# A four-layer trunk: feature-major products for SwiGLU, DeltaNet and RWKV's receptance, a triangle product for the RWKV decay, and the first norm's shift and scale in two halves

## The chip, the cores and the metric

The kernel runs on one core of one Trainium2 chip. The metric is the device time of one execution in microseconds (us); a run's time is compared with that of the kernel before on the same chip. The engines are TensorE (PE, with its weight loads shown as PEld), VectorE (DVE), ScalarE (ACT), GpSimd (POOL) and SyncE (SP, which only issues DMAs here). TensorE writes its products to PSUM, which has eight banks of 128 x 512 fp32.

## The reference, cut to what matters

Two streams of 128 tokens and 1024 features (a context and a latent) pass four layers. Each layer is a token mixer (DeltaNet, neighbourhood attention, latent attention, RWKV) and a SwiGLU FFN, each as `x += gate * f(rmsnorm(x) * (1 + scale) + shift)`. All arrays are fp32.

```python
mp = jnp.split(s_ctx @ ada_w[l] + ada_b[l], 6, -1)      # shift, scale, gate; shift, scale, gate
hp = modulate(rmsnorm(yp, norm_mix[l]), mp[0], mp[1])
...
q, k, v, z = jnp.split(h @ w_in, 4, -1)                 # DeltaNet, 4 x 1024 columns
qkv = jax.nn.silu(dwconv_centred(jnp.concatenate([q, k, v], -1), conv_w))   # 3 taps along the tokens
...
w = -jax.nn.softplus(-(w0[:, None, None, :] + lora(xm[3], w1, w2, jnp.tanh))) - 0.5   # RWKV, two directions
decay = jnp.exp(-jnp.exp(w.astype(F32)))
...
yp = yp + mp[5] * swiglu(modulate(rmsnorm(yp, norm_ffn[l]), mp[3], mp[4]), ffn_w_in[l], ffn_w_out[l])
```

The FFN goes from 1024 to 2 x 2816 features and back. The two streams are the two "groups" s = 0 and 1 below.

## The kernel before, in words

**Recording and planning.** The kernel's methods don't issue instructions; they record them on a tape (class Tape, line 64). Plan (line 1652) gives every instruction an estimated cost, orders all of them over the five engines by a list schedule with priorities (forwards, line 1787; backwards, line 1927), repeats this ROUNDS = 9 times with WAIT = 1800 ns (how long an engine may be kept for a more urgent instruction), and trunk_kernel (line 2040) issues the order with the shortest planned end. emit (line 2009) issues every instruction from one line, so all rows of the trace have line 2032 and all tiles the name v; groups are told apart by shape. Tiles come from fixed pools (ROOM, line 501): 25 of 1024 columns, 28 of 512, three of 2048 for ada_w, and 7 + 1 PSUM banks.

**Products in fp32r.** A weight block of 2 x 128 rows and 512 columns is loaded by SP and split into hi and lo (split, line 261: a ScalarE copy to fp32r and a VectorE subtraction, both 1024 columns). linear (line 296) holds the normalised tokens (128 features x 128 tokens of one group, hi and lo) stationary and streams 512 weight columns. For each row block k and group s it issues three products, x_hi w_hi, x_hi w_lo and x_lo w_hi, into one bank, 128 tokens x 512 features. Group 0 runs some steps ahead of group 1 (order, line 284; lags FIN, IN). linear_k (line 323) does the same over rows for FFN-out, with 2 x 2 banks. Plain fp32 products (RWKV's projections, the ada products) go through PE in two passes, each a matmul of its own in the trace; an fp32r product and a transpose are one.

**FFN** (ffn_, line 453). Chunks of 512 hidden features come in pairs, value and gate; the SiLU of the first is kept, the second multiplied by it, and to_T (line 360) turns the 128 x 512 result round with four PE transposes before it is split into hi and lo as the stationary operand of FFN-out: 11 x 4 = 44 transposes of 128 x 128 a layer.

**DeltaNet** (deltanet_, line 637). After the norm come a gate product (24 fp32r products, weights stationary, 256 columns of tokens) and linear over eight chunks: q, k, v and z, two chunks each. evac (line 733) copies a q, k or v chunk of one group from its bank, transposes it to feature-major (4), applies the three taps (per 128 features one ScalarE copy and two VectorE operations over 127 tokens), a SiLU, transposes back (4) and copies; q and k also get their squares summed. Then the triangular inverse for all heads runs on VectorE as one chain of 62 small operations between two pairs of 1024-wide stream transposes (inverse_base and substitute, lines 519 and 535).

**Shift and scale** (ada_group, line 217). A group g is 2048 of the 6144 columns of ada_w[l]: for each of eight row blocks four products, 32 rows of conditions stationary, 512 columns each, side by side in four column groups of the array. Group 0 of layer 0 is made in setup (line 176) from 16 loads of 1024 columns; the others by fill (line 1989), one 2048-column load for a row block, after each mixer's projections.

**RWKV** (rwkv_, line 1188). project (line 1283) makes k, r and v as plain fp32 products through linear_k, 512 columns each; features (line 1296) transposes r (16). rw_decays (line 1402) makes, for a half g of the features and a direction d, the decay's pre-activation by products of 64 rows x 256 columns, a tanh, an addition, a running sum along the tokens by two VectorE scans of 512, a subtraction of the value at the middle token, and exponentials. A half's keys, products and triangular inverse follow; the second half's inverse comes late in the layer.

Of the kernel before, what the change touches and what calls it, by code (L numbers as in the profile page):

```python
# [96 lines left out]
class Trunk:  # L97
# [78 lines left out]
    def setup(self):  # L176
# [18 lines left out]
        self.ada_group(0, 0, 1024, "b")  # L195
# [21 lines left out]
    def ada_group(self, l, g, width=2048, kind="ada"):  # L217
# [8 lines left out]
        n = width // 512  # L226
        for k in range(KD):
            for h in range(4 // n):
                w = self.g([128, width], kind=kind)
                at = g * 2048 + h * width  # L230
                nc.sync.dma_start(w, I["ada_w"][l, k * 128:(k + 1) * 128, at:at + width])
                for i in range(n):
                    j = h * n + i
                    nc.tensor.matmul(p[32 * j:32 * j + 32, :], self.cT[:, k, :], w[:, i * 512:i * 512 + 512],
                                     start=(k == 0), stop=(k == KD - 1), tile_position=(0, 32 * j))
                self.free(w)
# [13 lines left out]
    def ada_col(self, l, part, s):  # L250

        n = 2 * part
        return self.ada[l][:, n // 4, :, s].rearrange("p (c j) -> p j c", j=4)[:, n % 4:n % 4 + 2]
# [68 lines left out]

    def linear_k(self, W, xs, evac, lags=None, done=None, whole=False):
# [54 lines left out]
    def normed(self, l, which, s, more=None):  # L378
# [4 lines left out]
        with self.scope():  # L383
# [3 lines left out]
            nc.vector.scalar_tensor_tensor(gs, self.ada_col(l, 3 * which + 1, s), 1.0,  # L387
                                           self.gcol[:, which, l, :].rearrange("p (j c) -> p j c", j=2),
                                           op0=OP.add, op1=OP.mult)
            sh = self.ada_col(l, 3 * which, s)  # L390
            for g in range(2):
                xn = self.g([128, 512])
# [9 lines left out]
                yield g, p, gs[:, g, :], sh[:, g, :]  # L402
# [50 lines left out]
    def ffn_(self, l):  # L453
# [5 lines left out]
        chunks = []  # L459
        for c in range(5):  # L460
            chunks += [[(c * 512, c * 512 + 512)], [(FF + c * 512, FF + c * 512 + 512)]]
        chunks += [[(2560, FF), (FF + 2560, 2 * FF)]]
        sil = {}

        def evac(ci, s, ps):
            if ci < 10 and ci % 2 == 0:
# [6 lines left out]
            with self.scope():  # L473
                m = self.g([128, 512])
                if ci < 10:
                    nc.vector.tensor_tensor(m, ps, sil[s], op=OP.mult)
                    self.free(sil[s])
                    n = 4
                else:
                    t = self.g([128, 512])  # L480
                    nc.scalar.activation(t[:, :256], ps[:, :256], AF.Silu)
                    nc.vector.tensor_tensor(m[:, :256], ps[:, 256:], t[:, :256], op=OP.mult)
                    n = 2
                self.to_T(m, n, hid[c][0][:, :n, s, :], hid[c][1][:, :n, s, :])
        self.linear(W, chunks, xs, evac, FIN)
# [23 lines left out]
ROUNDS = 9  # L509
WAIT = 1800.0  # L510
# [5 lines left out]
class DeltaNet:  # L516
# [120 lines left out]
    def deltanet_(self, l):  # L637
# [95 lines left out]
        def evac(ci, s, ps):  # L733
            which, half = ci // 2, ci % 2
            if which == 3:
                nc.scalar.activation(zs[s][half].rearrange("p a b -> p (a b)"), ps, AF.Silu)
                return
            with self.scope():
                tok = self.g([128, 512])
                nc.scalar.activation(tok, ps, AF.Copy)  # L740
                p = self.ps()
                for i in range(4):
                    nc.tensor.transpose(p[:, i * 128:(i + 1) * 128], tok[:, i * 128:(i + 1) * 128], self.ident)
                x = p.rearrange("p (a b) -> p a b", b=128)
                cv = self.g([128, 4, 128])
                for i in range(4):
                    c = ci * 4 + i
                    nc.scalar.activation(cv[:, i], x[:, i], AF.Copy, scale=cw[:, 1, c:c + 1])
                    nc.vector.scalar_tensor_tensor(cv[:, i, 1:], x[:, i, :127], cw[:, 0, c:c + 1], cv[:, i, 1:], op0=OP.mult, op1=OP.add)
                    nc.vector.scalar_tensor_tensor(cv[:, i, :127], x[:, i, 1:], cw[:, 2, c:c + 1], cv[:, i, :127], op0=OP.mult, op1=OP.add)  # L750
                nc.scalar.activation(cv, cv, AF.Silu)
                p = self.ps()
                for i in range(4):
                    nc.tensor.transpose(p[:, i * 128:(i + 1) * 128], cv[:, i], self.ident)
                h0 = half * 4
                dst = (qk[s][which][:, h0:h0 + 4] if which < 2 else V[s][half]).rearrange("p a b -> p (a b)")
                nc.scalar.activation(dst, p, AF.Copy)
                if which < 2:
                    sq = self.g([128, 512])
                    nc.scalar.activation(sq, p, AF.Square)  # L760
                    nc.vector.tensor_reduce(ss[:, s, which, h0:h0 + 4], sq.rearrange("p (a b) -> p a b", b=128), axis=AX.X, op=OP.add)
            if ci == 3:
                unit(s)
            if ci == 5 and s == 1:
# [34 lines left out]
        self.linear(I["dn_w_in"][j], [[(c * 512, c * 512 + 512)] for c in range(8)], xs, evac, IN)  # L799
# [380 lines left out]
class Rwkv:  # L1180
# [7 lines left out]
    def rwkv_(self, l):  # L1188
# [4 lines left out]
        r = self.g([96, 128])  # L1193
        for at, n, v in ((0, 48, I["rw_mu"][j].rearrange("i (k p) -> (i k) p", p=128)),
                         (48, 8, I["rw_k_a"][j].rearrange("(k p) -> k p", p=128)),
                         (56, 8, I["rw_r_k"][j].rearrange("(k e) d -> k (e d)", e=2)),
                         (64, 16, I["rw_w0"][j].rearrange("z (k p) -> (z k) p", p=128)),
                         (80, 16, I["rw_a0"][j].rearrange("z (k p) -> (z k) p", p=128))):
            nc.gpsimd.dma_start(r[at:at + n], v)
        p = self.ps()  # L1200
        nc.tensor.transpose(p[:, :96], r, self.ident[:96, :96])
        self.free(r)
        cols = self.g([128, 96])
        nc.vector.tensor_copy(cols, p[:, :96])
        mu = cols[:, 0:48].rearrange("p (i k) -> p i k", k=8)

        nc.vector.tensor_scalar(cols[:, 64:96], cols[:, 64:96], 0.5, None, op0=OP.mult)
# [3 lines left out]
        self.rw_b0 = {"w": cols[:, 64:80].rearrange("p (z k) -> p z k", z=2), "a": cols[:, 80:96].rearrange("p (z k) -> p z k", z=2)}  # L1211
# [35 lines left out]
        wa = self.g([128, 2, 2, 128])  # L1247

        def lora(i, nm):
# [14 lines left out]
            t = hid[nm] = wa[:, "wa".index(nm)] if nm != "g" else self.g([128, 2, 128])  # L1264
# [5 lines left out]

        self.seg = self.g([128, 512])
        nc.gpsimd.memset(self.seg, 1.0)
        nc.gpsimd.memset(self.seg[:, ::128], 0.0)
        w2 = [{}, {}]
        for g in range(2):
            for nm in "wa":
                w2[g][nm] = self.g([128, 512])
                nc.gpsimd.dma_start(w2[g][nm], I[f"rw_{nm}2"][j].rearrange("z r n -> (z r) n")[:, g * 512:g * 512 + 512])
# [64 lines left out]
        lora(4, "a")  # L1343
        k = project(1, mk, KLAGS)
# [25 lines left out]
        r = project(0, mr, RLAGS)  # L1370
# [6 lines left out]
        rT = features(r)  # L1377
# [24 lines left out]
    def rw_decays(self, g, d, hid, w2):  # L1402
# [5 lines left out]
        act = {}  # L1408
        for nm in "wa":
            o = self.g([128, 4, 2, 128])  # L1410
            for h in range(2):
                p = self.ps()
                for i in range(2):
                    nc.tensor.matmul(p[:, i * 256:i * 256 + 256], w2[nm][rows, (2 * h + i) * 128:(2 * h + i + 1) * 128],
                                     hid[nm][rows].rearrange("p s t -> p (s t)"), start=True, stop=True, tile_position=(64 * d, 0))
                for i in range(2):
                    c = g * 4 + 2 * h + i
                    nc.scalar.activation(o[:, 2 * h + i].rearrange("p s t -> p (s t)"), p[:, i * 256:i * 256 + 256], AF.Tanh,
                                         bias=self.rw_b0[nm][:, d, c:c + 1], scale=0.5)
            act[nm] = o  # L1420
        sg, al = act["w"], act["a"]
        seq = lambda t: t.rearrange("p c s t -> p (c s) t")

        cm = self.g([128, 4, 2, 128])
        fl = lambda t: t.rearrange("p c s t -> p (c s t)")
        nc.vector.tensor_scalar(fl(sg), fl(sg), 1.0, None, op0=OP.add)
        a, b = (fl(sg), fl(cm)) if d == 0 else (fl(sg)[:, ::-1], fl(cm)[:, ::-1])
        shp = [128, 8, 128]
        for h in (0, 512):
            nc.vector.tensor_tensor_scan(b[:, h:h + 512], self.seg, a[:, h:h + 512], 0.0, op0=OP.mult, op1=OP.add)  # L1430
        mid = self.g([128, 8])
        nc.vector.tensor_copy(mid, seq(cm)[:, :, 63 + d])
# [628 lines left out]
```

## Time and profile before

| | |
|---|---|
| median of 3 runs | 1683.51 us (1679.96 to 1689.08) |
| the profiled execution | 1688.48 us, span 1686.7 us |
| PE busy | 1587.1 us, 9396 matmuls |
| VectorE, ScalarE busy | 1128.2 us, 830.3 us |
| loaded from HBM | 328.25 MB |
| granted TensorE clock, mean | 0.969 |

The profile is of one execution. A matmul's listed duration is its latency; matmuls overlap, so what one costs in a dense run is the step from start to start. "x" stands before a count. Times in timelines are from the span's start; a row there merges matmuls that follow each other and names the first one's shape.

### The profile page before, as it was taken

The numbers are of one execution on the slowest core, as the hardware profiler recorded it, in microseconds if no ns is written. First come the engines' busy times: TensorE is split into PE (matmuls) and PEld (weight loads), VectorE is DVE, ScalarE is ACT, GpSimd is POOL, SyncE is SP. The second block draws the span as 40 slices with busy tenths as digits, with TensorE's granted clock in tenths as the row PEclk, the third lists the DMA queues.
The fourth block names the chain that finished last, engine by engine and source line by source line (L and its number), as shares of the span: only waits on it lengthen the run. The fifth ranks groups of instructions, "written<-read, shape, count | busy, mean of one in ns | idle before, by whom it ended". The sixth has DMA issues, their size and how long they took to land.

```text
span 1686.7 us, 24968 instructions
## 1 busy us (share of the span) xinstructions
PE 1587.1 (94%) x9396; PEld 1206.5 (72%) x9396; DVE 1128.2 (67%) x2364; ACT 830.3 (49%) x1466; POOL 63.3 (4%) x109
## 2 busy tenths in 40 slices
PE   6999689999999899999998999999999499999998
PEld 2877267888767658887775688886657378878886
DVE  4788868545486675445798854548797878675554
ACT  4798166434455664444565644433545432354443
POOL 2001010000002000000000000001010010000000
PEclk9999899999999999999999999999998779999999
DMA  9665888545658684455767854557120452335553
GB/s 364 226 215 195 325 307 319 200 147 183 208 215 269 195 299 158 169 175 204 249 215 255 334 165 174 187 200 253 59 101 10 166 195 82 114 119 178 164 193 130
DMA packets 130601, 333.79 MB, mean 198 GB/s; under 512 B 18321, under 2 KB 32466, under 8 KB 119216
## 3 DMA queue, kind: packets, MB, share of 16 engines
q1 hardware_dynamic: 123888, 311.33, 52.4%
q0 software_dynamic: 6592, 20.86, 4.2%
q8 instruction: 74, 1.21, 0.3%
q14 instruction: 47, 0.39, 0.1%
HBM read 328.25 MB, written 3.90 MB: 197 GB/s over the span
## 4 chain that ended last, share of the span: by engine, by line
PE 73%; DVE 12%; DMA 8%; ACT 5%; issue 2%; SPq 0%; ACTq 0%; DVEq 0%
PE v L2032 73%; DVE v L2032 12%; DMA v<-ada_w 5%; ACT v L2032 4%; DMA v<-ffn_w_out 2%; DMA v<-na_w_qkv 1%; DMA v<-dn_w_in 1%; ACT L2032 0%; DMA v<-ffn_w_in 0%; SPq L2032 0%; ACTq L2057 0%; ACTq L2032 0%; DVEq L2032 0%
## 5 line engine op out<-in xcount | busy, mean ns | idle before, releaser
L2032 PE MATMUL v<-v,v 128*128 128x512 f32 (+13 forms) x9364 | 1582.6, 369 | 94.1 <-DVE v L2032 44.5
L2032 PEld LDWEIGHTS v<-v,v 128*128 128x128 f32 (+6 forms) x9364 | 1200.4, 170 | 473.2 <-issue 148.7
L2032 DVE TENSOR_TENSOR v<-v,v 128x512 f32<-128x512 f32 (+19 forms) x1271 | 864.4, 705 | 477.5 <-ACT v L2032 280.8
L2032 ACT ACTIVATE v<-v 128x512 f32<-128x512 f32 (+9 forms) x989 | 679.1, 721 | 797.2 <-PE v L2032 373.6
L2032 ACT ACTIVATE v<-v,v 128x128 f32<-128x128 f32 (+2 forms) x212 | 77.3, 413 | 30.4 <-PE v L2032 12.5
L2032 DVE SCALAR_TENSOR_TENSOR v<-v,v,v 128x127 f32<-128x127 f32 (+4 forms) x200 | 66.9, 381 | 7.1 <-ACT v L2032 6.1
L2032 ACT ACTIVATE v<-v,v,v 128x128 f32<-128x128 f32 (+2 forms) x136 | 55.4, 476 | 23.6 <-DVE v L2032 23.3
L2032 DVE TENSOR_REDUCE v<-v 128x4 f32<-128x512 f32 (+4 forms) x76 | 47.1, 626 | 18.0 <-PE v L2032 12.9
L2032 POOL DMA_DIRECT2D v<-v x22 | 11.8, 535 | 780.5 <-PE v L2032 633.9
L2032 DVE TENSOR_SCALAR v<-v 128x1 int32<-128x1 int32 (+9 forms) x194 | 32.8, 175 | 9.1 <-ACT v L2032 6.1
L2032 DVE SCALAR_TENSOR_TENSOR v<-v,v 128x1 f32<-128x1 f32 (+7 forms) x156 | 32.6, 218 | 4.8 <-ACT v L2032 2.2
L2032 ACT ACT_TABLE_LOAD x22 | 28.2, 1283 | 2.4 <-DVE v L2032 1.4
L2032 POOL MEMSET v<- 128x512 f32 (+3 forms) x26 | 15.6, 618 | 330.4 <-PE v L2032 182.4
L2032 DVE SCALAR_TENSOR_TENSOR v<-v 128x1 f32<-128x1 f32 (+4 forms) x171 | 26.2, 159 | 2.5
L2032 DVE TENSOR_SCALAR v<-v,v,v 128x128 f32<-128x128 f32 x64 | 25.0, 404 | 2.0 <-PE v L2032 1.5
L2032 DVE STREAM_TRANSPOSE v<-v 128x1024 f32<-128x1024 f32 x12 | 23.4, 2003 | 3.8 <-ACT v L2032 3.6
L2032 DVE TENSOR_SCALAR v<-v,v 128x512 f32<-128x512 f32 (+2 forms) x68 | 24.6, 395 | 0.4
L2032 DVE TENSOR_TENSOR v<-v 128x1 f32<-128x1 f32 (+4 forms) x74 | 11.7, 160 | 10.9 <-ACT v L2032 9.7
L2032 DVE COPY v<-v 128x32 f32<-128x32 f32 (+9 forms) x34 | 7.5, 223 | 12.8 <-PE v L2032 12.6
L2032 ACT ACTIVATION_READ_ACCUMULATOR v<-v,v 128x1 f32 x64 | 13.3, 208 | 0.0
L2032 DVE TENSOR_TENSOR_SCAN v<-v,v 128x512 f32<-128x512 f32 x8 | 9.2, 1206 | 0.1
L2032 PE MATMUL v<-v 128*128 128x256 f32 x32 | 8.0, 378 | 0.0
(39 smaller groups left out, 62.5 us busy)
## 6 DMA issues: line engine op xcount, KB each, us to landing
v<-ada_w SPq DMA_DIRECT2D x88, 1024.0 KB
v<-ffn_w_in SPq DMA_DIRECT2D x160, 512.0 KB
v<-ffn_w_out SPq DMA_DIRECT2D x88, 512.0 KB
v<-dn_w_in SPq DMA_DIRECT2D x32, 512.0 KB
v<-na_w_qkv SPq DMA_DIRECT2D x24, 512.0 KB
v<-rw_w_rkv SPq DMA_DIRECT2D x24, 512.0 KB
v<-v POOLq DMA_DIRECT2D x20, 512.0 KB, 7.0
v<-ada_w SPq DMA_DIRECT2D x16, 512.0 KB
```

The source lines that it names most:

```text
L2032: ins = getattr(getattr(nc, engine), method)(*[real(a) for a in args], **{k: real(a) for k, a in kw.items()}).ins
```

## The change

Five things are edited.

- **linear_T**, new: the weights (hi or lo, 128 x 128) are the stationary operand and the 2 x 128 tokens of both groups the moving one, 256 columns, so that a chunk of 512 features comes out feature-major in two banks. It takes all chunks of the FFN but the first pair (TM = 1), and q, k and v of DeltaNet; z stays with linear. With `early` = 2 the first two DeltaNet chunks are done in two halves of the rows.
- **The evacuations** behind it work on both groups at once: DeltaNet's lose the copy and the first four transposes, the FFN's lose to_T.
- **ada_start**: the first norm's shift and scale come in two halves of the features, each with its own eight loads of 2 x 512 columns, its biases and two column groups of PE; normed takes its scale and shift by halves.
- **RWKV**: r is projected with the weights stationary (project_T) and comes out feature-major; the decay's pre-activation is a token-major product with the bias as a row of ones, and the running sum along the tokens a product with a triangle whose middle column is subtracted beforehand (rw_tri). The value at the middle token is set to 1 by POOL.
- **Planning**: ROUNDS = 14 with each of WAITS = (900, 3000), so 28 orders to choose from.

```diff
-        self.ada_group(0, 0, 1024, "b")
+        self.ada_first = [self.c([128, 4, 2, 2]) for _ in range(2)]
+        for j in range(2):
+            self.ada_start(j)
...
+    def ada_start(self, j):
+        nc, I = self.nc, self.I
+        half = lambda a: a[:, 0:2048].rearrange("k (q j n) -> k q j n", q=2, j=2)[:, :, j]
+        b = self.g([64, 512])
+        nc.gpsimd.memset(b, 0.0)
+        for m in range(2):
+            nc.sync.dma_start(b[m::32], half(I["ada_b"][0:1]).rearrange("o q n -> (o q) n"))
+        p = self.ps()
+        for k in range(KD):
+            w = self.g([128, 2, 512])
+            nc.sync.dma_start(w, half(I["ada_w"][0, k * 128:(k + 1) * 128]))
+            for q in range(2):
+                nc.tensor.matmul(p[32 * q:32 * q + 32, :], self.cT[:, k, :], w[:, q], start=(k == 0), stop=(k == KD - 1),
+                                 tile_position=(0, 32 * q))
+            self.free(w)
...
+    def linear_T(self, W, chunks, ht, evac, early=0):
+        nc = self.nc
+        nk = W.shape[0] // 128
+        spans = [(ci, h * nk // 2, nk // 2) for h in range(2) for ci in range(early)] + [(ci, 0, nk) for ci in range(early, len(chunks))]
+        acc = {}
+        for ci, at, n in spans:
...
+            if at == 0:
+                acc[ci] = [self.ps() for _ in range(width // 256)]
+            banks = acc[ci]
+            for k0 in range(at, at + n, 2):
+                hi, lo = self.weight([W[k0 * 128:(k0 + 2) * 128, a:b] for a, b in pieces], 2, width)
+                for kk in range(2):
+                    k = k0 + kk
+                    xh, xl = [ht[x][k // 4][:, k % 4].rearrange("p s t -> p (s t)") for x in range(2)]
+                    for i in range(width // 128):
+                        o = banks[i // 2][:, i % 2 * 256:i % 2 * 256 + 256]
+                        c = slice(i * 128, i * 128 + 128)
+                        nc.tensor.matmul(o, hi[:, kk, c], xh, start=(k == 0 and i % 2 == 0), stop=False)
+                        nc.tensor.matmul(o, hi[:, kk, c], xl, start=False, stop=False)
+                        nc.tensor.matmul(o, lo[:, kk, c], xh, start=False, stop=(k == nk - 1 and i % 2 == 1))
+                self.free(hi, lo)
+            if at + n == nk:
+                evac(ci, banks)
...
-        self.linear(W, chunks, xs, evac, FIN)
+        self.linear(W, [[x] for c in range(TM) for x in pair(c)], xs, evac, FIN)
...
+        self.linear_T(W, [x for c in range(TM, 5) for x in pair(c)] + [[(2560, FF), (FF + 2560, 2 * FF)]], ht, evac)
...
-                tok = self.g([128, 512])
-                nc.scalar.activation(tok, ps, AF.Copy)
-                p = self.ps()
-                for i in range(4):
-                    nc.tensor.transpose(p[:, i * 128:(i + 1) * 128], tok[:, i * 128:(i + 1) * 128], self.ident)
...
+                    x = banks[i // 2].rearrange("p (a s t) -> p a s t", a=2, s=2)[:, i % 2]
+                    nc.scalar.activation(cv[:, i], x, AF.Copy, scale=cw[:, 1, c:c + 1])
+                    nc.vector.scalar_tensor_tensor(cv[:, i, :, 1:], x[:, :, :127], cw[:, 0, c:c + 1], cv[:, i, :, 1:], op0=OP.mult, op1=OP.add)
+                    nc.vector.scalar_tensor_tensor(cv[:, i, :, :127], x[:, :, 1:], cw[:, 2, c:c + 1], cv[:, i, :, :127], op0=OP.mult, op1=OP.add)
                 nc.scalar.activation(cv, cv, AF.Silu)
...
-        self.linear(I["dn_w_in"][j], [[(c * 512, c * 512 + 512)] for c in range(8)], xs, evac, IN)
+        self.linear_T(W, [(c * 512, c * 512 + 512) for c in range(6)], ht, evac, EARLY)
+        self.linear(W, [[(c * 512, c * 512 + 512)] for c in (6, 7)], xs, gating, IN)
...
-        r = project(0, mr, RLAGS)
+        rT = project_T(0, mr)
...
-            nc.vector.tensor_tensor_scan(b[:, h:h + 512], self.seg, a[:, h:h + 512], 0.0, op0=OP.mult, op1=OP.add)
...
+            nc.tensor.matmul(p, hid["w"][d][:, s], w2["w"][d], start=True, stop=True)
+            with self.scope():
+                sg = self.g([128, 512])
+                nc.scalar.activation(sg, p, AF.Tanh, scale=0.5)
+                nc.vector.tensor_scalar(sg, sg, 1.0, None, op0=OP.add)
+                q = self.ps()
+                for c in range(4):
+                    nc.tensor.matmul(q[:, c * 128:c * 128 + 128], sg[:, c * 128:c * 128 + 128], self.rw_tri[:, d], start=True, stop=True)
...
+            nc.gpsimd.memset(AR[s][:, :, 1, m:m + 1], 1.0)
+            nc.gpsimd.memset(cm[:, :, s, m:m + 1], 1.0)
...
-    _, order, turns, _ = min(Plan(tape).best(ROUNDS, (WAIT,)), key=lambda x: x[0])
+    _, order, turns, _ = min(Plan(tape).best(ROUNDS, WAITS), key=lambda x: x[0])
```

RWKV's second-layer weights and bias rows of the decay are laid into one 128-row tile per half and direction by four memsets and ten POOL loads, where four loads (and one of the bias with the layer's other columns) were.

## Rows read from the trace of the kernel before

**Rows 1.** The page's first part: busy us, share, instructions

```profile
PE 1587.1 (94%) x9396; PEld 1206.5 (72%) x9396; DVE 1128.2 (67%) x2364; ACT 830.3 (49%) x1466; POOL 63.3 (4%) x109
```

**Rows 2.** Busy time by stretches; PE, PEld, DVE, ACT, POOL, clock, DMA, GB/s

```profile
0.00:42.20 42.20, 26.06 (x105) 8.90 (x106) 17.28 (x53) 18.11 (x38) 9.70 (x21) 0.94 0.98 364
...
37.00:43.50 6.50, 5.13 (x22) 4.46 (x21) 5.21 (x8) 6.47 (x15) 0.00 (x0) 0.50 1.05 401
...
42.00:168.00 126.00, 124.35 (x655) 95.84 (x654) 103.69 (x240) 108.18 (x213) 6.87 (x10) 0.99 0.61 212
...
168.70:210.90 42.20, 26.06 (x351) 12.17 (x351) 34.46 (x102) 7.86 (x13) 1.23 (x3) 0.84 0.87 324
...
295.00:420.00 125.00, 125.00 (x567) 102.24 (x566) 61.78 (x64) 51.02 (x63) 1.07 (x2) 1.00 0.50 173
...
1100.00:1311.00 211.00, 210.29 (x1270) 140.57 (x1268) 160.56 (x324) 93.31 (x199) 10.32 (x13) 0.98 0.35 125
...
1326.00:1352.00 26.00, 4.29 (x29) 2.16 (x28) 23.74 (x65) 0.39 (x1) 0.00 (x0) 0.63 0.41 155
```

**Rows 3.** The chain of waits: start us, length us, what

```profile
163.97 3.95 DVE v L2032 x2
...
194.24 9.24 DMA v<-ada_w
```

**Rows 4.** PE's timeline, runs of like matmuls: start us, length us

```profile
1494.57 69.75 PE L2032 MATMUL v<-v,v 128*128 128x512 f32 x301
...
43.66 0.51 PE L2032 MATMUL v<-v,v 128*128 128x256 f32 x3
...
44.00 0.40 PE L2032 MATMUL v<-v,v 128*128 128x256 f32 x2
...
44.24 0.39 PE L2032 MATMUL v<-v,v 128*128 128x512 f32 x1
...
838.16 4.40 PE L2032 MATMUL v<-v,v 128*128 128x288 f32 x32
```

**Rows 5.** Groups by form, PE, 295-420 us: busy us, mean ns | idle

```profile
L2032 PE MATMUL v<-v,v 128*128 128x512 f32 x523 | 122.2, 393 | 0.0
```

**Rows 6.** Groups by form, ScalarE and VectorE, 50 to 165 us

```profile
L2032 ACT ACTIVATE v<-v,v 128x128 f32<-128x128 f32 x96 | 31.4, 379 | 4.2 <-DVE v L2032 3.1
...
L2032 ACT ACTIVATE v<-v 128x512 f32<-128x512 f32 x53 | 29.8, 603 | 0.9 <-PE v L2032 0.6
...
L2032 ACT ACT_TABLE_LOAD x13 | 16.7, 1283 | 1.5 <-DVE v L2032 1.4
...
L2032 DVE SCALAR_TENSOR_TENSOR v<-v,v,v 128x127 f32<-128x127 f32 x96 | 29.2, 344 | 6.5 <-ACT v L2032 5.7
```

**Rows 7.** Groups by form, VectorE, the whole span

```profile
L2032 DVE SCALAR_TENSOR_TENSOR v<-v,v,v 128x256 f32<-128x256 f32 x42 | 17.5, 478 | 0.1
```

**Rows 8.** PE's timeline, the start

```profile
23.83 1.05 PE L2032 MATMUL v<-v,v 128*32 128x512 f32 x4 [0.23 <-DMA v<-ada_w]
...
30.32 1.05 PE L2032 MATMUL v<-v,v 128*32 128x512 f32 x4 [0.25 <-DMA v<-ada_w]
...
38.85 11.38 PE L2032 MATMUL v<-v,v 128*128 128x512 f32 x50 [1.37 <-DVE v L2032]
```

**Rows 9.** Groups by form, VectorE, 1185-1206 us (RWKV, first decays)

```profile
L2032 DVE TENSOR_TENSOR_SCAN v<-v,v 128x512 f32<-128x512 f32 x4 | 4.6, 1201 | 0.0
...
L2032 DVE TENSOR_TENSOR v<-v,v 128x1024 f32<-128x1024 f32 x2 | 2.4, 1216 | 0.0
...
L2032 DVE TENSOR_SCALAR v<-v 128x1024 f32<-128x1024 f32 x2 | 1.4, 694 | 1.3 <-ACT v L2032 1.3
```

**Rows 10.** PE's timeline: fp32 passes of 512, of 128, 64-row of 256

```profile
1160.58 19.91 PE L2032 MATMUL v<-v,v 128*128 128x512 f32 x46
...
226.55 5.62 PE L2032 MATMUL v<-v,v 128*128 128x128 f32 x48
...
1193.75 1.78 PE L2032 MATMUL v<-v,v 64*128 64x256 f32 x14
```

More of the change, by code (lines that the diff above doesn't have):

```diff
@@ L225, in ada_group @@
         p = self.ps("back")
-        n = width // 512
         for k in range(KD):
[L228 to L236, printed above, removed]
+            w = self.g([128, 2048])
+            nc.sync.dma_start(w, I["ada_w"][l, k * 128:(k + 1) * 128, g * 2048:g * 2048 + 2048])
+            for j in range(4):
+                nc.tensor.matmul(p[32 * j:32 * j + 32, :], self.cT[:, k, :], w[:, j * 512:j * 512 + 512],
+                                 start=(k == 0), stop=(k == KD - 1), tile_position=(0, 32 * j))
+            self.free(w)
         s = self.g([128, 512])
@@ L458, in ffn_ @@
         hid = []
[L459 to L462, printed above, removed]
+        pair = lambda c: [(c * 512, c * 512 + 512), (FF + c * 512, FF + c * 512 + 512)]
         sil = {}
         def evac(ci, s, ps):
-            if ci < 10 and ci % 2 == 0:
+            if ci % 2 == 0:
                 sil[s] = self.g([128, 512])
@@ L1343, in rwkv_, with project_T @@
         lora(4, "a")
+        def project_T(i, m):
+            W = I["rw_w_rkv"][j, i]
+            acc = [self.ps() for _ in range(4)]
+            for k in range(KD):
+                w = self.raw_weight([W[k * 128:(k + 1) * 128, :]], 1, 1024)
+                x = m[k // 4][:, k % 4].rearrange("p s t -> p (s t)")
+                for b in range(8):
+                    nc.tensor.matmul(acc[b // 2][:, b % 2 * 256:b % 2 * 256 + 256], w[:, 0, b * 128:b * 128 + 128], x,
+                                     start=(k == 0 and b % 2 == 0), stop=(k == KD - 1 and b % 2 == 1))
+                self.free(w)
+                if k % 4 == 3:
+                    self.free(m[k // 4])
+            out = [self.g([128, 4, 2, 128]) for _ in range(2)]
+            for b in range(4):
+                nc.scalar.activation(out[b // 2][:, b % 2 * 2:b % 2 * 2 + 2], acc[b].rearrange("p (a s t) -> p a s t", a=2, s=2), AF.Copy)
+            return out
         k = project(1, mk, KLAGS)
@@ L1407, in rw_decays @@
         rows = slice(64 * d, 64 * d + 64)
[L1408 to L1420, printed above, removed]
@@ new lines, in rw_decays @@
+            nc.scalar.activation(cm[:, :, s], q, AF.Exp, scale=KAPPA / 2)
+            nc.scalar.activation(first[:, :, s], q[:, :, m], AF.Exp, scale=-KAPPA / 2)
+            nc.scalar.activation(fc[:, :, s, 0], q[:, :, m], AF.Exp, scale=KAPPA / 2)
+            nc.scalar.activation(fc[:, :, s, 1], q[:, :, end], AF.Exp, scale=-KAPPA / 2)
+            nc.gpsimd.memset(AR[s][:, :, 1, m:m + 1], 1.0)
+            nc.gpsimd.memset(cm[:, :, s, m:m + 1], 1.0)
+        al = self.g([128, 4, 2, 128])
+        for h in range(2):
+            p = self.ps()
+            for i in range(2):
+                nc.tensor.matmul(p[:, i * 256:i * 256 + 256], w2["a"][rows, (2 * h + i) * 128:(2 * h + i + 1) * 128],
+                                 hid["a"][rows].rearrange("p s t -> p (s t)"), start=True, stop=True, tile_position=(64 * d, 0))
+            for i in range(2):
+                c = g * 4 + 2 * h + i
+                nc.scalar.activation(al[:, 2 * h + i].rearrange("p s t -> p (s t)"), p[:, i * 256:i * 256 + 256], AF.Tanh,
+                                     bias=self.rw_a0[:, d, c:c + 1], scale=0.5)
```

179 lines of the change are left out of this document (103 added, 76 removed).

## The prediction, made before the changed kernel was run

> **What bounds the kernel now.** The page comes first: TensorE (PE) is busy 94% of the span, VectorE 67%, ScalarE 49% [rows 1]. So the first question is what the change does to PE's own work, the second what it does where PE is idle, 99.6 us in all (1686.7 - 1587.1). The table by stretches, read next, shows three such places: 16.1 us in the first 42, 16.1 between 169 and 211 us (DeltaNet), 21.7 between 1326 and 1352 us (RWKV) [rows 2]. The chain of waits names what ends them: in DeltaNet the transposes with which VectorE opens the triangular inverse at 164 us, later a 9.2 us load of ada_w [rows 3]; in RWKV VectorE works 23.74 of those 26 us, again on an inverse [rows 2]. Elsewhere PE hardly waits; in the first FFN it is busy for 125.00 us of 125 [rows 2].
>
> The page is of an execution of 1688.5 us, 1686.7 of them span. The sum is made against it, and its difference taken from the median of the three runs, 1683.5 us, which lies 5.0 us lower.
>
> **Narrow matmuls instead of wide ones.** linear_T makes the weights the stationary operand and the 2 x 128 tokens the moving one: a product of 512 columns becomes two of 256. What counts is the step between starts; the listed mean is a latency. 301 products of 512 last 69.75 us, less one latency of 0.39 that is 0.231 us a step [rows 4]. The 256-wide form, fp32r weights stationary and the same order hi, hi, lo, stands once in the trace, in the DeltaNet gate. Five of its products lie between 43.66 and 44.24, where the wide ones begin: 0.116 us a step; the three before 44.00 give 0.113, the two after it 0.120 [rows 4]. A width between speaks for the same: 288 columns step by 0.1324, and the slope from there to 512 (0.0988 for 224 columns) leads to 0.118 at 256 [rows 4]. I take 0.117, and keep 0.113 and 0.120 for the range.
>
> FFN: in each layer eight chunks of 512 and the last of 2 x 256 go over, 9 x 96 = 864 narrow products, 101.1 us, for 432 wide ones, 99.9: 1.2 us lost. The hidden values now come out transposed, which removes 36 of a layer's 44 transposes. In the 125 us of the first FFN 523 wide products take 120.9, which leaves 4.1 for the 44 transposes, 0.093 each [rows 2, 5]; 36 are 3.35 us. Net -2.2 a layer, **-8.6 us** in four (-22.5 at 0.113, +1.7 at 0.120). The evacuations keep their elements; ScalarE and VectorE are busy 51 and 62 of these 125 us [rows 2], so they cost nothing. Without that cover a late evacuation would hold two banks, and PE with them. The second token group's lag goes, but the first pair of chunks keeps it.
>
> DeltaNet: 576 narrow for 288 wide, 67.4 for 66.5 us, and 48 transposes fewer, 4.5 us: **-3.6 us** of PE.
>
> **DeltaNet's other engines.** ScalarE is busy 108 of the 126 us to the inverse [rows 2], with 13 table loads of 1.283, 53 activations of 512 at 0.603 and 96 of 128 at 0.379 [rows 6]. The change drops 12 of the 512-wide copies (7.2 us), makes 24 convolution copies of 256 (between these rows 0.45 each, 10.9 us) out of 48 of 128 (18.2), and does both groups' SiLUs at once, 6 for 12, which saves between none and six table loads (0 to 7.7): 14 to 22 us. On VectorE 48 fused operations of 2 x 127 replace 96 of 127: at 0.478, the 256-wide row, for 0.344 that is 22.9 for 33.0, -10 us [rows 6, 7]. PE is full before the inverse too (124.35 of 126), so an earlier inverse pays only by the work that the plan can leave under it: the z chunks, 96 wide products, 22 us of PE, but with eight weight splits on VectorE, 10 us at the 1.216 of a subtraction of 1024 [rows 9], the engine that does the inverse. What is late next is ada_w: DMA is at 0.87 in that stretch [rows 2]. Of 16.1 us idle I take **-7 us**, near the middle because both reasons hold; the bounds are 0 and -16.
>
> **The start.** The 16 loads of ada_w's first group end at about 30.3 us, two for each row block, whose four products take 1.05 us and are hidden under them. Six blocks' products begin from 23.83 to 30.32, a load each, 1.30 us apart; norm and transposes follow, and PE runs without pause from 38.85 [rows 8]. Now eight loads come first, 10.4 us fewer, so the norm's first half is there at 28.5 or sooner. Waiting then are four half-chunks' weights, 96 narrow products, 11 us, and the second half's ada products, eight at about 1.05, 8.4 us, which no longer lie under an idle PE. PE is thus full from 28.5 with 8.4 us more to do: -2 us, a little more if the half norm is faster than the whole. The eight later loads stand on SP's queue before the other weights, the same bytes, with two bias loads more; PE has its 11 us meanwhile. From 37.0 to 43.5 us the granted clock was 0.50, 1.2 GHz [rows 2], after some microseconds with little PE work; if the early products run so, they take about 20 us and the gain is gone. **-2.5 us**, between +3 and -8. The order is the planner's: if it doesn't put the halves so, the term is 0.
>
> **RWKV.** The decay's running sum goes from VectorE's scan to a product with a triangle. For each half and direction VectorE loses an addition of 1024 (0.694), two scans (1.201 each) and a subtraction of 1024 (1.216), 4.3 us, four times, and gains two additions of 512, at half of 0.694; with some small copies and set-up that is -14 us [rows 9]. PE gains, for each half, direction and group, one plain fp32 product of 512, two passes of 0.43 (46 in 19.91 us), and four of 128, two passes of 0.113 (48 in 5.62 us): 8 x 1.76 = 14.1 us. It loses 32 passes of 64 x 256 at 0.107 (14 in 1.78 us), 3.4 us, and r's 16 transposes, 1.5 [rows 10]: **+9 us of PE**. r's projection turned round has the same columns, and costs the same. POOL gets about five DMAs and some memsets more ahead of the layer, and sixteen one-column memsets between the exponentials and the keys; it is 4% busy [rows 1], so I take 0; the sixteen as long as VectorE's smallest large operation here, 0.694, and all on the chain, would be +11. PE is busy 210.29 of the 211 us to 1311 [rows 2], so the +9 is on the path unless as much other work moves under the second inverse, where PE has 4.29 of 26 us. VectorE, 160.56 of those 211 us, is what this inverse waits for, and a queue lighter by 14 us should bring it forward by about what PE loses: **0 us**, between +11 and -13.
>
> **The plan.** 28 orders are tried instead of 9, and the untouched layers are ordered anew. No row prices it. Outside the three places 45.7 us of idle PE are scattered; a better or worse order could move a fifth of that, so I take 0, within 10.
>
> Sum: -8.6 - 3.6 - 7 - 2.5 + 0 = -21.7 us: 1666.8 for the profiled execution, **1662 us** from the median. About 0.5%, 8.4 us, is what a measurement of this kernel can tell from no change.
>
> **Rivals.** (1) *The idle closes wholly*: -8.6 - 3.6 - 2.5 - 16.1 in DeltaNet - (21.7 - 9) in RWKV = -43.5: 1640. For it: ScalarE and VectorE get lighter just there. Against: VectorE does the inverse itself, and most of what could fill the gap needs it too.
> (2) *The relief buys nothing*: ada_w's loads end the wait in DeltaNet as they do at 194 us [rows 3], and RWKV pays its 9 us. -8.6 - 3.6 - 2.5 + 9 = -6: 1678, no change. For it: DMA at 0.87 and PE full for 211 us. Against: the inverse starts as late as 164 us because of ScalarE's and VectorE's queues, which do shrink.
> (3) *Slower, by a part of each narrow product that doesn't shrink with its columns.* 4032 of them run. At 0.1245 us the forecast has become -21.7 + 4032 x 0.0075 = +8.5, and from there it is slower; at 0.126 it is +14.6, 1698; at the 0.1324 of 288 columns, the worst row near it, +40. For it: the clean steps are only five and rise to 0.120, and products of 128 columns step by 0.113 [rows 10], not by a quarter of 0.231: under something like that a load of 128 weight columns may not hide. Against: 256, 288 and 512 lie on one line.
> On this the Trainium skill (TensorE: Matmul & The Clock Gate, Back-to-back issue gap) gives sustained spacings of 81 ns at 128 columns and 131 ns at 512; by an estimate from that page, on the line between them, 256 would cost 98, two of them 65 more than one wide, and the 2016 pairs 130 us, some 1790 us. The trace does not agree with the page: 512 columns step by 231 here.
>
> **Chances.** Forecast 0.58, (1) 0.13, (2) 0.18, (3) 0.11. Faster by over 0.5%: the forecast and (1), less a sliver at the forecast's edge, 0.70. Within: (2) and the sliver, 0.19. Slower: 0.11. The range, 1640 to 1684, takes in the bounds of the terms as far as they don't all fall to one side, and leaves out (3) and half of (1).
>
> **What would show it.** The narrow run's step in the FFN, 0.117 (wrong from 0.1245); FFN stretches still full, each 2 us shorter; fewer than 13 table loads in DeltaNet, and the inverse's transposes some 10 us before 164; PE's first long run before 31 us; no scans, and a second gap in RWKV under 15 us. An idle gap that only moves, or PE busy for more than 1587 us, would prove the sum wrong.

## The result, and the profile after

The changed kernel takes 1655.1 us (median of 4 runs, 1652.7 to 1659.6) beside 1681.7 for the kernel before: ratio 0.9844 [0.9814, 0.9875], 26.6 us less. That is near the 1662 forecast and inside the range. The experiments say something less flattering: 10 to 13 us of the gain came from a term that the sum had put at 0.

The page's first part, after (the profiled execution: 1659.6 us, span 1657.8, granted clock 0.978 over the span, 0.969 before):

```profile
span 1657.8 us, 28812 instructions
...
PE 1577.0 (95%) x11320; PEld 1295.8 (78%) x11320; DVE 1097.0 (66%) x2294; ACT 811.7 (49%) x1405; POOL 71.7 (4%) x137
```

Beside [rows 1] PE is busy 10.1 us less and idle 18.8 us less (80.8 for 99.6). The columns of the next view are those of [rows 2]; the kernel before, cut where each layer's last residual is done (DeltaNet, FFN, neighbourhood attention, FFN, latent attention, FFN, RWKV, FFN):

```profile
0.00:271.40 271.40, 232.96 (x1641) 160.30 (x1645) 197.44 (x496) 169.85 (x319) 24.64 (x47) 0.96 0.77 278
...
469.20:619.80 150.60, 139.84 (x800) 106.08 (x798) 111.12 (x255) 86.79 (x181) 9.98 (x14) 0.95 0.70 230
...
1154.70:1485.60 330.90, 303.25 (x2621) 219.61 (x2620) 268.03 (x564) 137.60 (x294) 14.82 (x24) 0.93 0.34 117
```

The same stages after:

```profile
0.00:254.30 254.30, 226.96 (x1867) 167.62 (x1867) 190.24 (x448) 154.69 (x274) 25.45 (x47) 0.97 0.82 289
254.30:458.40 204.10, 201.76 (x1341) 176.13 (x1337) 107.04 (x140) 91.19 (x116) 1.10 (x2) 1.00 0.66 225
458.40:590.60 132.20, 129.85 (x763) 101.64 (x759) 109.03 (x256) 86.66 (x179) 10.50 (x15) 1.00 0.70 224
...
1122.00:1455.20 333.20, 310.38 (x2745) 234.87 (x2741) 254.00 (x551) 134.39 (x302) 16.60 (x40) 0.94 0.36 124
```

A stage's length can be split into PE's idle time, the time lost because PE worked at 1.2 instead of 2.4 GHz (an estimate: half of its busy time in stretches of clock 0.50), and the rest, its work at the full clock. Split so, the two profiles differ by:

| us, after less before | length | idle | lost at 0.50 | work |
|---|---|---|---|---|
| DeltaNet | -17.1 | -11.1 | -2.2 | -3.8 |
| FFN 1 + neighbourhood attention | -12.1 | -7.9 | -5.4 | +1.2 |
| FFN 2 + latent attention | -7.3 | +0.9 | -2.0 | -6.2 |
| FFN 3 | +3.8 | +2.2 | 0 | +1.6 |
| RWKV | +2.3 | -4.8 | -1.6 | +8.7 |
| FFN 4 and the end | +1.5 | +1.9 | +0.1 | -0.5 |
| span | -28.9 | -18.8 | -11.1 | +1.0 |

A layer and its FFN stand together where ada_w's products moved over the border between them. The attention layers, whose code nobody touched, are shorter with their FFNs by 19 us. Not all of it is gained: 32 matmuls of ada_w went from the latent attention and its FFN over to FFN 3, an estimate of 4 to 8 us (132 such matmuls are busy for 17.9 us in RWKV after, four for 1.05 at the start [rows 8]). Most of it is idle time and the clock, though, and that is where the experiments begin.

### The profile page after: what moved, and what is told of

Same layout as the page of the kernel before. It is cut to its first block, busy times and chain, and to the rows that moved or that the text cites. A ratio compares the mean times of both kernels' runs of the same rounds, so it can differ in the third digit from the quotient of the medians.

```text
span 1657.8 us, 28812 instructions
## 1 busy us (share of the span) xinstructions
PE 1577.0 (95%) x11320; PEld 1295.8 (78%) x11320; DVE 1097.0 (66%) x2294; ACT 811.7 (49%) x1405; POOL 71.7 (4%) x137
## 5 line engine op out<-in xcount | busy, mean ns | idle before, releaser
L2133 PE MATMUL v<-v,v 128*128 128x256 f32 (+12 forms) x11288 | 1571.5, 331 | 74.9 <-DVE v L2133 34.2
L2133 PEld LDWEIGHTS v<-v,v 128*128 128x128 f32 (+8 forms) x11288 | 1290.1, 173 | 354.0 <-issue 123.9
L2133 DVE TENSOR_TENSOR v<-v,v 128x512 f32<-128x512 f32 (+16 forms) x1244 | 856.1, 714 | 480.9 <-ACT v L2133 328.3
L2133 ACT ACTIVATE v<-v 128x1024 fp32r<-128x1024 f32 (+14 forms) x972 | 674.6, 732 | 782.1 <-PE v L2133 316.1
L2133 ACT ACTIVATE v<-v,v 128x128 f32<-128x128 f32 (+2 forms) x172 | 65.6, 434 | 21.7 <-DVE v L2133 14.0
L2133 DVE SCALAR_TENSOR_TENSOR v<-v,v,v 128x128 f32<-128x128 f32 (+4 forms) x152 | 59.1, 446 | 6.0 <-ACT v L2133 3.8
L2133 DVE TENSOR_SCALAR v<-v 128x1 int32<-128x1 int32 (+11 forms) x202 | 35.0, 177 | 6.2 <-ACT v L2133 3.7
L2133 DVE SCALAR_TENSOR_TENSOR v<-v,v 128x4 f32<-128x4 f32 (+6 forms) x172 | 34.0, 211 | 5.2 <-ACT v L2133 3.3
L2133 POOL MEMSET v<- 128x512 f32 (+6 forms) x49 | 21.4, 446 | 365.5 <-DVE v L2133 143.1
L2133 DVE COPY v<-v 128x32 f32<-128x32 f32 (+7 forms) x23 | 4.9, 211 | 13.3 <-PE v L2133 13.1
L2133 POOL DMA_DIRECT2D v<-rw_w x10 | 6.0, 601 | 59.4 <-DVE v L2133 58.5
```

The source lines that it names most:

```text
L2133: ins = getattr(getattr(nc, engine), method)(*[real(a) for a in args], **{k: real(a) for k, a in kw.items()}).ins
```

## The experiments

Each ratio is to runs of the kernel before on the same chip. What the expectations call the search is the two plan settings.

**1, 2. The plan alone, and the edits without it.** The kernel before with the new settings, and the changed kernel with the old ones:

```diff
 b_plan, from the kernel before
-ROUNDS = 9
-WAIT = 1800.0
+ROUNDS = 14
+WAITS = (900.0, 3000.0)
 a_plan9, from the changed kernel
-ROUNDS = 14
-WAITS = (900.0, 3000.0)
+ROUNDS = 9
+WAITS = (1800.0,)
```

> The kernel before with the planning of the change alone (14 rounds, two waits, 28 orders), everything else as before. Theory A (the gain is the sum of PE work saved and idle closed in the edited stages): 1681 us, within 5 of the kernel before. Rival B (the new planning is worth much of it, since the attention layer, where nothing was edited, lost 18.5 us and 8.5 us of its PE idle): 1671 us or less, and the attention layer, from the end of the first FFN to the end of its own residual, takes about 135 us instead of 150.7.

> The changed kernel with the planning of the kernel before (9 rounds, one wait of 1800 ns). Theory A: 1655 us, within 5 of the changed kernel. Rival B: 1665 us or more, with the attention layer back at about 150 us.

The profiled run of a kernel can lie 10 us from its median (a_plan9: 1682.1 for 1671.1), so differences of stages below some 5 us are not read.

Measured: the plan alone 1673.3 us, 0.9940 [0.9913, 0.9966], 10 us less; the edits with the old search 1671.1 us, 0.9922 [0.9893, 0.9952], 13 us less. The changed kernel has 0.9844: the edits bring 0.0078 of the time and the new search on top of them another 0.0078, 13 us each. Counted the other way round, the search brings 10 us and the edits on top of it 16. What the search finds can be seen in the neighbourhood attention. PE's timeline there, before (start, length, what, and in brackets the idle time ahead of it and what ended it):

```profile
544.67 3.21 PE L2032 MATMUL v<-v,v 128*128 128x512 f32 x22
554.17 0.80 PE L2032 MATMUL v<-v,v 128*128 128x512 f32 x1 [6.29 <-ACT v L2032]
```

The same layer in b_plan, by the view of stretches:

```profile
468.60:605.80 137.20, 133.53 (x788) 101.51 (x786) 108.79 (x252) 83.42 (x177) 9.99 (x15) 0.99 0.70 237
```

The 6.29 us in which PE waited for ScalarE is gone with no edit to any layer; idle falls from 10.8 to 3.7 us, and the granted clock, which read 0.50 from inside that wait on (552 to 559 us), is 0.99 over the stage. In a_plan9 the layer takes 141.8 us, not the 150 that rival B expected. DeltaNet moves with the search too: its stage in b_plan and in a_plan9 is

```profile
0.00:269.80 269.80, 238.85 (x1630) 164.77 (x1630) 195.89 (x497) 168.70 (x320) 25.06 (x47) 0.94 0.75 274
0.00:264.10 264.10, 230.01 (x1871) 171.45 (x1871) 190.33 (x449) 161.72 (x280) 24.81 (x47) 0.95 0.78 280
```

so PE is idle for 30.9 us with the search alone and 34.1 with the edits alone, for 38.4 before. Over the whole span b_plan's profile has 14.4 us less idle time than before's, 6.3 less lost at 0.50, and 4.2 more of work.

**3 to 6. One edit taken out of the changed kernel, new search kept.** a_noF has the FFN of before, a_noD the wide q, k, v of before (and so no half-row products), a_noR the RWKV of before, a_noS the whole first group and no half-row products:

```diff
 a_noF, in the FFN
-        self.linear_T(W, [x for c in range(TM, 5) for x in pair(c)] + [[(2560, FF), (FF + 2560, 2 * FF)]], ht, evac)
+        self.linear(W, chunks, xs, evac, FIN)
 a_noD, in DeltaNet
-        self.linear_T(W, [(c * 512, c * 512 + 512) for c in range(6)], ht, evac, EARLY)
+        self.linear(I["dn_w_in"][j], [[(c * 512, c * 512 + 512)] for c in range(8)], xs, evac, IN)
 a_noR, in RWKV
-        rT = project_T(0, mr)
+        r = project(0, mr, RLAGS)
 a_noS, in the start
-        for j in range(2):
-            self.ada_start(j)
+        self.ada_group(0, 0, 1024, "b")
...
-EARLY = 2
+EARLY = 0
```

> The changed kernel with the FFN as before (token-major products, 44 transposes a layer), the rest of the change kept. Theory A, with the narrow step now read as 0.118 us: the four FFNs' change is worth 1.1 us of PE each, so 1659.5 us, and not below 1655. Rival C (the FFN stages got longer by 6.3, 3.9 and 1.1 us in the changed kernel because the form costs something): 1650 us or less.

> The changed kernel with DeltaNet's q, k and v made and evacuated as before (the first norm's halves and all else kept, but no products by halves of the rows). Theory A: ScalarE's and VectorE's lighter queues bring the inverse forward by 10 us, so here it starts at about 161 us instead of 153.5, ScalarE loads 13 or more tables before it, and the time is 1665 us. Rival D (the start in halves is what brought the inverse forward): the inverse starts by 156 us and the time is 1657 us.

> The changed kernel with the RWKV layer as before (r token-major and transposed, decays by VectorE's scan), all else kept, same search. Theory A (the PE work added there, 9 us, and VectorE's relief cancel): 1655 us, within 5 of the changed kernel, PE busy some 9 us less than its 1577 and the RWKV stage near 333 us. Rival E (the relief is what counts): 1665 us or more. Rival G (where the search puts the work around the second inverse decides, not the edit): the stage is off by 10 us or more either way, with the time at half clock in it changed by as much.

> The changed kernel with the first norm's shift and scale in one piece again and no products by halves of the rows; all else kept, same search. Theory A: the start is worth 2.5 us: 1657.6 us, PE's long run begins at about 38.9 us, and the first inverse at 156 us instead of 153.5. Rival D (the start is worth what the DeltaNet stage gained, since without the feature-major q, k and v the time moved by 3 us only): the first inverse at 161 us or later and 1663 us or more.

Measured (the granted clock is the median over a kernel's runs; the last two columns are of the profiled execution):

| kernel | us | ratio | clock | DeltaNet, us | RWKV, us (at clock 0.50) |
|---|---|---|---|---|---|
| before | 1681.7 | 1 | 0.969 | 271.4 | 330.8 (48) |
| after | 1655.1 | 0.9844 [0.9814, 0.9875] | 0.979 | 254.3 | 333.1 (38) |
| a_noF | 1690.6 | 1.0051 [1.0025, 1.0077] | 0.966 | 259.3 | 361.9 (79) |
| a_noD | 1657.9 | 0.9852 [0.9823, 0.9882] | 0.985 | 264.4 | 325.0 (17) |
| a_noR | 1679.2 | 0.9969 [0.9943, 0.9995] | 0.970 | 262.3 | 347.5 (65) |
| a_noS | 1677.5 | 0.9961 [0.9936, 0.9986] | 0.977 | 269.1 | 343.7 (55) |

a_noF came out as neither theory had it. a_noD has rival D's time, but theory A's inverse, at 161.18 us; a_noS has rival D's time and inverse, at 165.65. a_noR is rival G's: its RWKV stage is 14.4 us longer than after's, with 27 us more at 0.50.

Read as prices these say 35 us for the FFN, 3 for DeltaNet, 24 for RWKV, 22 for the start: 84 in all, of a gain of 27. They can't all be prices, and the profile of a_noF shows why. Outside DeltaNet and RWKV its profiled execution takes 1068.4 us (after: 1070.3), nearly the same; but its RWKV, the same code as after's, takes 28.8 us more. The stage and a stretch of it:

```profile
1125.20:1487.10 361.90, 341.83 (x2753) 257.42 (x2749) 253.87 (x554) 135.06 (x303) 15.48 (x38) 0.89 0.32 111
1330.00:1374.40 44.40, 42.19 (x440) 31.96 (x442) 28.41 (x58) 13.19 (x21) 2.13 (x4) 0.50 0.35 120
```

After, the stretch in the same place:

```profile
1310.80:1348.30 37.50, 25.97 (x260) 21.01 (x262) 35.76 (x82) 9.12 (x15) 0.53 (x1) 0.50 0.20 66
```

In both the clock falls to 0.50 while the second inverse runs, after some microseconds in which PE has short pieces of work between waits, and stays there through the small products that follow. After, it falls at 1310.8 us, 5 us ahead of the long wait (10.17 us, shown further down); in a_noF at 1330.0, 10 us behind this one:

```profile
1319.83 5.03 PE L2120 MATMUL v<-v,v 128*32 128x512 f32 x28 [6.10 <-DVE v L2120]
```

In a_noF 42.19 us of PE's work lie in that stretch, and 17.10 more in a second one from 1384.7 us; after, 25.97. So a leave-one-out run here measures the edit and a newly drawn order together, and the order can be worth more than the edit.

**7, 8. The same two edits under the old search.** a_noF9 and a_noR9 are a_noF and a_noR with the settings of a_plan9, their partner:

> The changed kernel with the FFN as before, and the search of the kernel before (9 rounds, 1800 ns); its partner with the new FFN and this search took 1671 us. Theory G (the 35 us that the old FFN cost under the new search are the order found for RWKV, 79 us of it at half clock, and not the FFN): 1668 to 1677 us, the four FFN stages within 5 us of the partner's 797, net of the ada products in them. Rival F (the feature-major FFN is itself worth 30 us): 1700 us or more.

> The changed kernel with the RWKV layer as before and the search of the kernel before; its partner with the new RWKV and this search took 1671 us. Theory A: 1671 us, within 5, the RWKV stage within 6 of the partner's 347. Rival G: the stage differs by 10 us or more, in the direction opposite to, or of another size than, that under the new search.

Measured: 1669.0 us, 0.9920 [0.9890, 0.9950], and 1674.0 us, 0.9942 [0.9916, 0.9968], for 0.9922 with both edits in. The times are theory G's and theory A's. The FFN's edit is worth nothing that shows here, where it was 35 us under the new search; RWKV's 3 us, within the intervals, where it was 24. The large prices belonged to the orders. The RWKV stage itself is rival G's here too. With the old code (a_noR9) and with the new one (a_plan9) it is

```profile
1142.00:1468.00 326.00, 308.00 (x2640) 219.27 (x2638) 265.75 (x567) 137.11 (x292) 15.17 (x24) 0.95 0.36 125
1131.40:1478.40 347.00, 326.21 (x2741) 244.23 (x2740) 250.77 (x548) 133.12 (x301) 16.12 (x39) 0.93 0.34 119
```

21 us shorter with the old code, where under the new search the old code's was 14.4 longer. The profiled run of a_plan9 lies 11 us above its median, which can be part of the 21, and a_noF9, with a_plan9's RWKV and search, has 332.7: the length of this stage is the order's.

**9, 10. The four FFNs alone.** The order is out of the way if the layers around are. Both with the old search, mixers left out, so the times are of four FFNs with their norms and ada_w:

```diff
 f_old (FFN of before), f_new (FFN of after)
-            mixers[l](l)
+            self.fill(l)
             self.ffn(l)
```

> The four FFNs alone: the four mixers are left out, the shift, scale and gate products stay; the FFN as before, first norm in halves, search of 9 rounds at 1800 ns. It is the base for its partner with the new FFN; about 4 x 198 us and a start of 40 to 70 us, 830 to 870 us.

> The same with the FFN of the change. Theory A at the step now read, 0.118 us: PE loses 1.1 us a layer, so 4.5 us less than the partner. The term as predicted (0.117): 8.6 us less. Rival A0 (the lost lag and later evacuations give it back as idle): within 2 us. Rival F (the form is worth what leaving it out cost): 30 us less.

Measured: 932.1 us (931.1 to 934.8), some 60 above what was expected of the base, and 929.2 (928.2 to 931.6), 2.9 less. The pages, f_old's first part and then f_new's:

```profile
PE 886.4 (95%) x4230; PEld 644.4 (69%) x4230; DVE 449.8 (48%) x597; ACT 368.2 (40%) x483; POOL 12.8 (1%) x29
```

```profile
PE 882.5 (95%) x5814; PEld 712.7 (77%) x5814; DVE 447.2 (48%) x573; ACT 366.3 (40%) x459; POOL 12.8 (1%) x29
```

PE is busy 3.9 us less, 1 a layer, and in these profiles (spans 929.3 and 926.7 us) 1.3 of them are given back as idle time. The granted clock was not quite the same, 0.986 and 0.982, mostly by the first 42 us (0.92 and 0.84): by the split above f_new lost 2.1 us more at 0.50, and its work at the full clock is 6.1 us less. The step is in the trace of the changed kernel, where a run of narrow products is this (PE's timeline, the second FFN):

```profile
636.35 20.82 PE L2133 MATMUL v<-v,v 128*128 128x256 f32 x175
```

Less one latency of 0.28 that is 0.118 us a step.

**11, 12. DeltaNet alone.** The first layer, its start and nothing else, old search:

```diff
 d_old, from the kernel before; d_new, from a_plan9
-        for l in range(4):
-            mixers[l](l)
-            self.ffn(l)
+        mixers[0](0)
```

> The kernel before with DeltaNet's mixer alone, its start and its three shift and scale groups; the FFNs and the other mixers are left out. Base for its partner; about 270 us, the inverse at 164 us.

> The same layer of the changed kernel, search of 9 rounds at 1800 ns as in the partner. Theory A (start -2.5, PE -3.6, idle -7): 13 us less than the partner, the inverse's transposes 10 us earlier. Rival H (the 17 us of the stage were the order's luck): within 4 us, with an inverse that starts within 3 us of the partner's.

Measured: 273.4 us (271.8 to 275.5) and 264.3 (263.1 to 266.0), 9.1 less. The view of stretches, d_old and then d_new:

```profile
0.00:42.00 42.00, 26.25 (x126) 8.55 (x127) 15.73 (x51) 16.88 (x37) 8.30 (x18) 1.00 0.97 368
42.00:155.00 113.00, 110.85 (x574) 86.72 (x572) 97.03 (x237) 99.66 (x194) 4.93 (x8) 1.00 0.61 208
```

```profile
0.00:42.00 42.00, 30.70 (x155) 12.72 (x156) 17.18 (x56) 18.09 (x37) 8.87 (x19) 1.00 0.99 355
42.00:155.00 113.00, 110.70 (x833) 94.79 (x832) 88.94 (x189) 91.10 (x158) 4.96 (x8) 1.00 0.74 269
```

The profiled spans are 272.1 and 262.2 us, PE's busy times 230.8 and 229.5: of the 9.9 us between these executions 1.3 are PE's busy time (by the split 2.5 less of work, 1.2 more lost at 0.50) and 8.6 idle time, and 4.4 of the idle time lay in the first 42 us (26.25 to 30.70 busy), where the half norm lets PE begin. ScalarE and VectorE are lighter by 8.6 and 8.1 us between 42 and 155, yet the inverse starts only 3.9 us earlier (158.9 for 162.8). In the full kernel, with the new search, it starts 10.4 us earlier, at 153.55; with the edits alone (a_plan9) or the search alone (b_plan) it hardly moves. It is the order that decides: a_noF9, with a_plan9's DeltaNet code and search, has it at 155.33. ScalarE's table loads, 50 to 160 us, d_old and d_new, and the inverse's first transposes in a_plan9 and b_plan:

```profile
L2030 ACT ACT_TABLE_LOAD x11 | 14.1, 1283 | 0.2
L2131 ACT ACT_TABLE_LOAD x13 | 16.7, 1283 | 1.9 <-DVE v L2131 1.8
...
162.76 3.86 DVE L2133 STREAM_TRANSPOSE v<-v 128x1024 f32<-128x1024 f32 x2 [0.51 <-ACT v L2133]
163.61 3.88 DVE L2032 STREAM_TRANSPOSE v<-v 128x1024 f32<-128x1024 f32 x2 [0.75 <-ACT v L2032]
```

## Why the prediction was right, and by what

Its total is right, in part by luck; its parts are less so. By the searches' runs the edits are worth 13 us (0.9893 to 0.9952, so 8 to 18) where the sum had 21.7, and the plan 13 where it had 0 (16 and 10 when the plan is counted first).

**The narrow step, and the FFN: the term was mis-sized.** I took 0.117, between the 0.116 of five products in a row at 43.66 us and the 0.118 of the line through 288 and 512 columns [rows 4]; it is 0.118. On 864 products that is 1 us a layer, so 1.1 gained and not 2.2: -4.4 for four. The runs of the FFNs alone show -3.9 of PE's busy time, an estimated -6.1 of work at the full clock, and -2.9 of time, for -8.6. On so small a margin the third digit of the step is the term; a run of 32 products was a better base than one of five. Rival 3 falls with it: of a narrow product hardly anything fails to shrink, since two of 0.118 stand beside one of 0.231. By an estimate on the line between the two spacings that the Trainium skill (TensorE: Matmul & The Clock Gate, Back-to-back issue gap) gives for 128 and 512 columns, 256 would take 98 ns; fp32r products of 256 columns take 118 here.

**The FFN's cover held.** In after's first FFN PE is busy 201.76 of 204.10 us with ScalarE at 91 and VectorE at 107, as forecast; the stretches are not each 2 us shorter, though, because ada_w's products were moved among them (72 matmuls in the first FFN for 36).

**DeltaNet and the start: right in kind, and the start shown.** PE's work there fell by 3.8 us in the profile of the full kernel (-3.6 forecast), idle time by 11.1 (-9.5 with the start), of which the search alone brings 7.5 in b_plan. Alone, the layer gained 9.1 for 13.1: its idle time fell by 8.6, but PE's work by 2.5 and its busy time by 1.3 only. ScalarE's forms between 50 and 154 us, after (columns as [rows 6]):

```profile
L2133 ACT ACTIVATE v<-v 128x512 f32<-128x512 f32 x30 | 16.0, 605 | 2.8 <-PE v L2133 2.8
L2133 ACT ACTIVATE v<-v,v 128x128 f32<-128x128 f32 x48 | 15.6, 391 | 0.2
L2133 ACT ACT_TABLE_LOAD x9 | 11.5, 1283 | 3.2 <-DVE v L2133 3.0
L2133 ACT ACTIVATE v<-v,v 128x256 f32<-128x256 f32 x24 | 10.8, 470 | 3.6 <-PE v L2133 2.2 <-DVE v L2133 1.1
```

The 24 copies of 256 at 0.470 (0.45 estimated) for 48 of 128 are as forecast. The nine table loads for 13 are not shown to be the edit's: alone the layer goes from 11 to 13, and a_plan9 has 13 between 50 us and its inverse. Over the whole stage ScalarE lost 15.2 us (14 to 22) and VectorE 7.2 (10); in a_plan9 they lost 8.1 and 7.1. The idle time that is left waits where it did, and that was the limit I gave. VectorE's and PE's timelines, after:

```profile
153.55 3.95 DVE L2133 STREAM_TRANSPOSE v<-v 128x1024 f32<-128x1024 f32 x2 [1.47 <-ACT v L2133]
```

```profile
149.43 19.10 PE L2133 MATMUL v<-v,v 128*32 128x512 f32 x123
178.24 2.79 PE L2133 MATMUL v<-v,v 128*32 128x512 f32 x12 [9.72 <-DVE v L2133]
```

The inverse begins 10.4 us earlier than in [rows 3]; PE works 15 us under it and then waits 9.72 us for VectorE. That start was forecast from ScalarE's and VectorE's lighter queues, and they alone do not give it: a_plan9 has them, and its inverse begins 1.2 us earlier. At the start, PE's first long run begins at 32.32 us, not before 31, for 38.85 [rows 8]:

```profile
30.93 1.05 PE L2133 MATMUL v<-v,v 128*32 128x512 f32 x4 [0.31 <-DMA v<-ada_w]
32.32 13.94 PE L2133 MATMUL v<-v,v 128*128 128x256 f32 x107 [0.34 <-DVE v L2133]
```

60 of the first group's 64 matmuls still run ahead of it, where the forecast had the second half's behind it (a row of 1.05 us there is one load's two products, in two passes each); 6.5 us are left of the gain. This gain doesn't hang on the order: in the eight kernels here with DeltaNet and the halves the run begins at 31.97 to 36.75 us, in the four with the first group whole at 38.05 to 42.54. The clock, 0.50 from 37.0 to 43.5 before [rows 2], stays at 1.00 up to 154 us after. How the 9.1 us divide between the start and the feature-major products was not isolated: a_noS and a_noD both lose 10 to 15 us of the DeltaNet stage, under other orders.

**RWKV: right in these two profiles, not shown beyond them.** PE's work rose by 8.7 us for 9, VectorE's fell by 14.0 for 14 (268.03 to 254.00; no scan is left), and the stage ended 2.3 us longer for 0. The second gap is 10.17 us for 21.89 (under 15 forecast), before and after:

```profile
1352.18 1.03 PE L2032 MATMUL v<-v,v 32*32 32x32 f32 x31 [21.89 <-DVE v L2032]
...
1325.99 1.11 PE L2133 MATMUL v<-v,v 64*64 64x64 f32 x8 [10.17 <-DVE v L2133]
```

It did not all close; idle fell by 4.8 us over the whole stage, since smaller waits opened, 3.5 us of them on ada_w. Nor is what closed shown to be the work of VectorE's lighter queue. The gap is as short with RWKV's old code, in a_noR and a_noR9:

```profile
1323.44 3.05 PE L2099 MATMUL v<-v,v 32*32 32x32 f32 x100 [10.46 <-DVE v L2099]
...
1319.79 5.38 PE L2099 MATMUL v<-v,v 128*32 128x512 f32 x28 [6.13 <-DVE v L2099]
```

Nor is the stage's 0 shown to hold: under the old search the new code takes 347.0 us in a_plan9 and 332.7 in a_noF9, for 330.9 before.

**The plan: the step that failed.** "No row prices it. ... I take 0, within 10." The runs show 10 us on the kernel before and 13 on the changed one. I had looked for its worth in a fifth of the scattered idle time, and left out the clock, which read 0.50 around the waits in the neighbourhood attention and in RWKV. In b_plan's profile the idle time alone is 14.4 us less, half of that in DeltaNet, and 6.3 more came back from stretches at 0.50. Of the 28.9 us between the spans before and after, 11.1 came back from such stretches, and no term of the sum held any of it. The plan also changed what the other terms brought: DeltaNet's idle time fell by 11.1 us with it, and in a_plan9 by 4.3 (38.4 to 34.1). That the total still came out is luck: two errors of opposite sign, the edits some 9 us too good and the plan 13 too poor. Rival 1 does not describe it either: the second gap in RWKV went from 21.89 to 10.17 us and DeltaNet's idle time from 38.4 to 27.3, neither wholly. Rival 2 describes the edits alone about as well as the forecast: their 13 us lie between its 6 and the forecast's 21.7, and in a_plan9 DeltaNet's inverse came only 1.2 us earlier and the RWKV stage was no shorter.

What stays open: RWKV's edit was not run alone, and its worth was 3 us under one search and 24 under the other; EARLY was not turned off by itself; which of the 28 orders the chip would like best is not known, and the planner takes the one with the shortest planned end. No variant beat the changed kernel.

## What to carry to other kernels

When one change edits a layer and the search that orders the whole program, run the search on the old program first, and price edits in isolated layers or under more than one search: taking one edit out re-draws every order, and under one fixed search it gave prices here that summed to three times the gain. Compare by stages, and split each into idle time, time at the lower clock and work. Take a step from the longest clean run, or from a line through wider ones, when the margin is one per cent of it.

## What the runs showed that was not expected

The time follows the granted clock from run to run of one and the same kernel: a_plan9's twelve runs go from 1662.5 us at a mean clock of 0.984 to 1684.7 at 0.970, and 63 runs of the kernel before that stood beside these kernels lie on a line of 1.27 us for each 0.001 (correlation -0.86). By that line, if it holds from one kernel to another, which no run shows, the step of the clock between the two kernels, 0.969 to 0.979, goes with some 13 of the 26.6 us; the split of the two profiles gave 11. In RWKV, where the clock falls while the second inverse runs, the time at 0.50 went from 17 to 79 us over kernels whose work in the layer is, by the split, 289 to 306 us.
